# Front pairs of a two-layer hybrid trunk: which steps stand behind the casts in the queues, and when the S1 tiles of the next pair are loaded

## The chip, the cores and the metric

The kernel runs on one core of one Trainium2 chip. A time is the device time of one execution in microseconds (us), and it is the median over several executions. A core has five engines with a queue each: TensorE (PE, matmuls, with the weight loads shown as PEld), VectorE (DVE), ScalarE (ACT), GpSimd (POOL) and SyncE (SP, which here only issues DMAs). Each works through its queue in the order written, and an instruction that waits for a semaphore holds up all behind it.

## The reference

Two layers, a sequence of 512 tokens, width 2048, float32. In each layer one projection `h @ w_in` gives all heads' inputs and gates, and one projection `@ w_out` brings their outputs back:

```
h = rmsnorm(x, g_pre)
z = h @ w_in
gq, gk, gv, gg, ga, aq, ak, av, ag = split_columns(z)
log_a = log_sigmoid(ga @ w_alpha + b_alpha) / 16
o_gla = rmsnorm(gla_chunk_causal(gq, gk, gv, log_a)) * silu(gg)
o_att = rmsnorm(chunk_band_attention(aq, ak, av, rel_bias)) * silu(ag)
y = concatenate([o_gla, o_att]) @ w_out
return x + rmsnorm(y, g_post)
```

## The kernel before

**Matmuls.** [...] For a weight tile the cast is made on ScalarE (`high`, `wh`, line 251) and the subtraction on VectorE (`low`, `wl`, line 257).

**Pairs.** Two blocks of 512 columns of `w_in` make a pair. Instead of eight block products, a pair takes seven (P1 to P7, after Strassen), of sums of weight blocks and of sums of token blocks. Each product is cut along the inner dimension into four jobs, c = 0 to 3, of 512 KB of weights and 12 matmuls. P5 and P6 add two weight tiles on VectorE first (line 240). The token sums S1 to S4 are made once per layer (`make_sums`, additions on line 764), split, and written to DRAM; P5 multiplies S1, P6 S2, P3 S4, P7 S3 and P4 A22.

**Front pairs.** Three pairs of each layer come first: pair 0 (AG0, AG1), pair 1 (GG0, GG1) and pair 2 (AV0, AV1). Their P1 and P2 form a head that needs no token sums:

```
HEAD = (("P1", 0), ("P1", 1), ("P2", 0), ("P2", 1), ("P1", 2), ("P2", 2))
```

Meanwhile the token steps, a generator that is advanced `rate` times a job (`pump`), prepare the token columns: in layer 0 each chunk is scaled by `g_pre` half on ScalarE and half on VectorE (lines 718 and 716), then split into high and low (lines 113 and 114). Then, pair by pair, come P5, the mixture of P6 and P3 (`MIDDLE`: P6 c0, P3 c0, P6 c1, P3 c1, P6 c2, P6 c3, P3 c2, P3 c3), P7 and P4.

**Copies between banks.** P1's result stays in PSUM banks "X", and is copied out (`copies("p1")`, line 432) before P2 adds onto the same banks. Before P4, the X banks are copied onto the Y banks (line 534), and P4 adds onto these. For P7's last and P4's first job the matmuls go token tile by token tile.

**Preparing ahead.** After a job, `ahead()` prepares the next: weight loads up to five jobs ahead, casts up to four, lows up to three, and loads of token sums (`bring`, line 230) up to four. Weight tiles lie in rings of four; a load waits until the tile four before it has been read.

**Order.** A scheduler places the instructions of each engine by a simulation of the program, by readiness, and by program order among those that are ready. The kernel adds edges: `issue_after(i)` puts an instruction behind `i` on its engine. `behind()` does that with the second to last cast and the second to last low traced so far, where the flag is set:

```
if in_front[0] and len(casts) > 1 and len(lows) > 1:
    with tc.issue_after(casts[-2]), tc.issue_after(lows[-2]):
        yield
```

All token steps go through it while `in_front[0]` is true, that is in all three front pairs, and so does `close`, what is done with a finished product (the copies too).

**S1 tiles.** Pairs 1 and 2 read S1 back from DRAM, 512 KB for each c, into four slots (g8, g11, g14, g15) used in turn by P5 c0 to c3, then by P6 c0, P3 c0, P6 c1 and P3 c1, then by the next pair's P5. `bring_next` issues those of the next pair after P7 c0 to c3, each behind the last weight load traced. The forget gate's steps (its last has lines 900 to 902) run beside pair 1 at `rate=0.25`.

Of the kernel before, what the change touches and what calls it, by code (L numbers as in the profile page):

```python
# [35 lines left out]
def hybrid_trunk(  # L36
# [13 lines left out]
    nc = tc.nc  # L50
# [85 lines left out]
    C_IN, C_END = (0, 1, 2, 3), (2, 3, 0, 1)  # L136
    MIDDLE = (("P6", 0), ("P3", 0), ("P6", 1), ("P3", 1), ("P6", 2), ("P6", 3), ("P3", 2), ("P3", 3))

    def products(cs, *names):
        return [(p, c) for p in names for c in cs]  # L140

    def middle(cs):
        return [(p, cs[i]) for p, i in MIDDLE]
# [5 lines left out]
    def early_rest(cs):  # L149
        return products(cs, "P5") + middle(cs) + products(cs, "P7", "P4")  # L150
# [11 lines left out]
    in_front = [False]  # L162

    @contextmanager
    def behind():
# [3 lines that stand above are left out]
        else:  # L169
            yield  # L170
# [94 lines left out]
    stream, infos_of = [], []  # L265
# [24 lines left out]
    def take(l, blk, kind, c):  # L290
        i = cursor[0]
        job = stream[i]
        assert (job.l, job.b0, job.kind, job.c) == (l, blk, kind, c)
        for what in ("load", "bring", "high", "low"):
            prepare(what, i + 1)
        cursor[0] += 1
        return job

    def ahead():
        i = cursor[0]  # L300
        for what, n in (("load", 3), ("high", 3), ("low", 3), ("load", 4), ("high", 4), ("load", 5), ("bring", 4)):
            if what in ("high", "low") and all(z.kind == "std" for z in stream[i + n - 2 : i + n]):
                n -= 1
            prepare(what, i + n)
# [26 lines left out]
    def drain():  # L331
        while tasks or delayed:
            pump(1)
# [72 lines left out]
    class Pair:  # L406
# [104 lines left out]
        def run(self, prods, rate=0.0, skip=0, after=None):  # L511
            pace = Pace(rate, skip)
            for k, c in prods:
                job = take(self.l, self.b0, k, c)
                self.matmuls(job, k, c)
                ahead()
                if c == self.last:
                    with behind():
                        self.close(k)
                if after is not None:  # L520
                    after(k, c)
                pace()

        def close(self, k):
            if k == "P1":
                self.copies("p1", self.acc["X"])
            elif k == "P5":
                self.copies("p5", self.acc["Y"])
            elif k == "P6":
                self.copies("x", self.acc["X"])  # L530
            else:
                if k == "P7" and self.seeded:
                    for t in range(2):
                        nc.scalar.copy(self.acc["Y"][t], self.acc["X"][t])  # L534
                for t in range(2):
                    self.finished(k, t)
                if k == "P7" and self.early and not self.seeded:
                    self.copies("x", self.acc["X"])
# [119 lines left out]
    def turn_norms():  # L658
        while turns:
            turns.pop(0)()  # L660
            yield
# [193 lines left out]
    def layer(l):  # L855
# [10 lines left out]
        def gate_consume(half):  # L866
            def f(j, h, t, src, comb):
                z = settled(src, comb)
                until(lambda: (l, h) in normed)
                gate(half, j, 2 * h + t, z, inv_rms(l, 2 * h + t))  # L870
            return f
# [97 lines left out]
        def av_consume(j, h, t, src, comb):  # L969
# [14 lines left out]
        front = [  # L984
            Pair(l, FRONT[0], gate_consume(1), scaled=False, **how),
            Pair(l, FRONT[1], gate_consume(0), scaled=False, x_bank=2, **how),
            Pair(l, FRONT[2], av_consume, keep=early_kept, **how),
        ]
        in_front[0] = True
        for n, (k, i) in enumerate(HEAD):  # L990
            front[i].run(products(C_IN, k), rate=2.7 if n < 2 and l == 0 else 1.9)
        if l == 0:
            tasks[0] = beside(tasks[0], first_norms(1), 2)
            tasks.append(load_forget_gate(0))
        tasks.append(turn_norms())
        def bring_next(i):
            def f(k, c):
                if k == "P7":
                    next(z for z in stream if z.pair is infos_of[l][i] and (z.kind, z.c) == ("P5", c)).bring()
            return f  # L1000

        front[0].open(0)
        front[0].run(early_rest(C_IN), rate=1.0, after=bring_next(1))
        drain()
        tasks.append(forget_gate())
        front[1].open(2)
        front[1].run(early_rest(C_IN), rate=0.25, after=bring_next(2))
        drain()
        act_table("natural_log_exp_and_others")
        av[0, 0] = slot(AVT[0][0], [2, 512])  # L1010
# [505 lines left out]
    for l in range(L):  # L1516
        layer(l)
# [57 lines left out]
```

## Time and profile before

| | |
|---|---|
| median of 3 runs | 1615.48 us (1614.38 to 1619.49) |
| profiled execution | 1618.52 us, span of its instructions 1616.7 us |
| TensorE busy | 1590.8 us (98%) |
| VectorE, ScalarE, GpSimd busy | 78%, 57%, 11% |
| DMA | 467.83 MB, mean 289 GB/s |
| TensorE's mean granted clock | 0.997 |

The span runs from the first to the last instruction. A row of the timeline gives start, duration, engine, line, operation, and output<-inputs by the program's names; in brackets stands how long the engine was idle before it and what released it. In layer 0 the front pairs take about the first 256 us, in layer 1 about the stretch from 811 to 1056 us.

### The profile page before, as it was taken

The page shows a single profiled execution, that of the slowest core. Times are in us where ns is not written, and L with a number is a line of the kernel's source. Part 1 is how long each engine was busy: PE and PEld are TensorE (multiplying, and loading weights), DVE is VectorE, ACT ScalarE, POOL GpSimd, SP SyncE. Part 2 cuts the span into 40 slices and gives each one's busy share as a digit, 9 for nine tenths or more (in the row PEclk, how much of TensorE's full clock was granted, in tenths as well). Part 3 has the DMA queues.
Part 4 walks back from the last instruction along what each step waited for, and adds up shares of the span by engine and source line. Part 5 has one row for each costly group of instructions (what it writes and reads, how often), then busy time and mean ns, then how long its engine had stood idle before and what let it go on. Part 6 is the DMA issues. An engine that isn't in the chain of part 4 may idle for free.

```text
span 1616.7 us, 24522 instructions
## 1 busy us (share of the span) xinstructions
PE 1590.8 (98%) x8818; PEld 1355.4 (84%) x8818; DVE 1257.7 (78%) x1580; ACT 923.4 (57%) x1534; POOL 181.5 (11%) x302
## 2 busy tenths in 40 slices
PE   8999999999999999999999999999999999999997
PEld 5787879999988887788887877899999888777886
DVE  6788787786877876778868878768778868866886
ACT  7575454456676544555675555445566765445543
POOL 1141000000101101310212100000000011013100
PEclk9999999999999999999999999999999999999999
DMA  9989777867868698799878789678588676979996
GB/s 365 370 282 363 287 244 260 294 208 270 294 212 288 225 344 308 269 379 331 344 242 322 282 313 340 227 244 298 184 310 295 213 273 237 356 240 342 374 322 223
DMA packets 150617, 467.83 MB, mean 289 GB/s; under 512 B 16492, under 2 KB 35956, under 8 KB 150496
## 3 DMA queue, kind: packets, MB, share of 16 engines
q1 hardware_dynamic: 127232, 385.79, 67.6%
q0 software_dynamic: 22688, 79.53, 12.8%
q8 instruction: 69, 1.13, 0.3%
q10 hardware_dynamic: 576, 0.95, 0.2%
q14 instruction: 52, 0.43, 0.1%
HBM read 393.01 MB, written 72.11 MB: 288 GB/s over the span
## 4 chain that ended last, share of the span: by engine, by line
PE 92%; DMA 4%; DVE 2%; issue 1%; ACT 1%; SPq 0%; DVEq 0%; POOLq 0%; ACTq 0%
PE mm L504 49%; PE mm L491 20%; PE mm L380 11%; DMA H<-in_w_dram 3%; PE ax L1087 2%; PE ax L504 1%; DMA raw<-in_w_dram 1%; PE ax L1070 1%; PE ax L1253 1%; PE ax L1287 1%; DVE wl L257 1%; PE ax L1049 1%; PE ax L1050 1%; PE ax L686 1%; PE ax L1048 1%
## 5 line engine op out<-in xcount | busy, mean ns | idle before, releaser
L251 ACT CAST wh<-raw 128x1024 fp32r<-128x1024 f32 x256 | 269.4, 1053 | 237.9 <-PE mm L504 111.5
L257 DVE TENSOR_TENSOR wl<-raw,wh 128x1024 fp32r<-128x1024 f32 x256 | 312.5, 1222 | 115.2 <-PE mm L504 43.0
L251 ACT CAST wh<-H 128x1024 fp32r<-128x1024 f32 x239 | 251.0, 1052 | 230.1 <-PE mm L504 88.0
L257 DVE TENSOR_TENSOR wl<-H,wh 128x1024 fp32r<-128x1024 f32 (+1 forms) x241 | 292.8, 1217 | 101.7 <-PE mm L504 44.0
L504 PE MATMUL mm<-wh,sa 128*128 128x512 f32 x1088 | 345.3, 392 | 2.0 <-ACT mm L534 2.0
L504 PE MATMUL mm<-wh,g 128*128 128x512 f32 x832 | 259.2, 391 | 0.0
L504 PEld LDWEIGHTS mm<-wh,sa 128*128 128x128 f32 x1088 | 203.2, 188 | 45.7 <-ACT mm L534 2.9
L491 PE MATMUL mm<-sa,wh 128*128 128x256 f32 x1280 | 235.9, 285 | 0.0
L504 PE MATMUL mm<-wh,a 128*128 128x512 f32 x704 | 229.4, 397 | 6.3 <-ACT a L113 5.2
L504 PE MATMUL mm<-wl,sa 128*128 128x512 f32 x544 | 212.5, 391 | 0.0
L240 DVE TENSOR_TENSOR H<-H,raw 128x1024 f32<-128x1024 f32 x160 | 194.2, 1220 | 18.3 <-DMA raw<-in_w_dram 9.0
L491 PEld LDWEIGHTS mm<-sa,wh 128*128 128x128 f32 x1280 | 199.3, 192 | 0.3
L504 PEld LDWEIGHTS mm<-wh,g 128*128 128x128 f32 x832 | 156.8, 189 | 32.7 <-ACT wh L251 0.3
L491 PE MATMUL mm<-sa,wl 128*128 128x256 f32 x640 | 181.0, 283 | 0.0
L504 PE MATMUL mm<-wl,g 128*128 128x512 f32 x416 | 163.2, 392 | 7.3 <-DVE wl L257 7.3
L504 PEld LDWEIGHTS mm<-wh,a 128*128 128x128 f32 x704 | 132.0, 189 | 39.5 <-ACT a L113 6.2
L504 PE MATMUL mm<-wl,a 128*128 128x512 f32 x352 | 138.8, 394 | 0.6 <-DVE wl L257 0.6
L491 PEld LDWEIGHTS mm<-sa,wl 128*128 128x128 f32 x640 | 122.3, 191 | 0.1
L504 PEld LDWEIGHTS mm<-wl,sa 128*128 128x128 f32 x544 | 102.2, 188 | 20.9
L504 PEld LDWEIGHTS mm<-wl,g 128*128 128x128 f32 x416 | 78.4, 189 | 26.5 <-DVE wl L257 10.1
L491 PE MATMUL mm<-a,wh 128*128 128x256 f32 x512 | 94.3, 285 | 0.0
L551 POOL TENSOR_TENSOR sm<-sm,cst 128x4 f32<-128x4 f32 (+2 forms) x40 | 49.0, 1225 | 326.6 <-DVE sm L1447 131.7
(208 smaller groups left out, 2271.9 us busy)
## 6 DMA issues: line engine op xcount, KB each, us to landing
raw<-in_w_dram SPq DMA_DIRECT2D x352, 512.0 KB, 5.5
sa<-S SPq DMA_DIRECT2D x128, 512.0 KB, 4.5
H<-in_w_dram SPq DMA_DIRECT2D x63, 512.0 KB, 5.9
S<-g POOLq DMA_DIRECT2D x32, 512.0 KB, 5.8
g<-S SPq DMA_DIRECT2D x32, 512.0 KB, 5.8
sa<-A SPq DMA_DIRECT2D x32, 512.0 KB, 5.9
oS<-g POOLq DMA_DIRECT2D x32, 512.0 KB, 6.1
sa<-oS SPq DMA_DIRECT2D x32, 512.0 KB, 5.1
```

What stands on the lines that cost most here:

```text
L240: nc.vector.tensor_tensor(out=h, in0=h, in1=r, op=ALU.add)
L251: last_cast[0] = nc.scalar.copy(self.wh, src).ins
L257: last_low[0] = nc.vector.tensor_tensor(out=self.wl[:, kk, :], in0=self.src[:, kk, :], in1=self.wh[:, kk, :].bitcast(F32), op=ALU.subtract ...
L380: mm = nc.tensor.matmul(pss[o], a[:, part, t], rhs[:, kk, :], start=(i == 0 and kk == 0 and m == 0), stop=(i == n - 1 and kk == 1 and m == 2),
L491: nc.tensor.matmul(dst, lhs[:, kk, f], a[:, part, tok], start=(fresh and kk == 0 and m == 0 and ft % 2 == 0), stop=(c == self.last and kk ...
L504: nc.tensor.matmul(out_ps[t], a[:, part, tok], rhs[:, kk, :], start=(fresh and kk == 0 and m == 0), stop=(c == self.last and kk == 1 and m ...
L551: return nc.gpsimd.tensor_tensor(out=out_r, in0=v, in1=mhalf[:, : v.shape[-1]], op=ALU.pow).ins
L686: mm = nc.tensor.matmul(gate_ps[l][g : g + 32, half * 256 : (half + 1) * 256], gate_w[l][:, kh * 8 + c * 2 + kk, :], full[half, c][:, kh, ...
L1048: nc.tensor.matmul(ps[:, :n], self.qh[:, t], self.kh[:, :n], start=True, stop=False)
L1049: nc.tensor.matmul(ps[:, :n], self.qh[:, t], self.kl[:, :n], start=False, stop=False)
L1050: nc.tensor.matmul(ps[:, :n], self.ql[:, t], self.kh[:, :n], start=False, stop=True)
L1087: nc.tensor.matmul(o, self.pt[i][:, j * P : (j + 1) * P], av[hd // 4, j // 2][:, j % 2, (hd % 4) * P : (hd % 4 + 1) * P], start=(j == 0), ...
```

## The change

1. The flag `in_front[0]` is set only from the third entry of the head on in layer 0 (in layer 1 from the first, as before). So in layer 0 the token steps beside P1 of pairs 0 and 1, eight jobs, get no edge.
2. The copies of P1's result and those of X onto Y before P4 move out of `close` and ahead of it, so they get no edge.
3. The S1 loads of the next pair are issued elsewhere: for pair 1 after P5 c1, P6 c0, P7 c0 and P7 c1 of pair 0; for pair 2 after P6 c1, P6 c2, P6 c3 and P3 c3 of pair 1.
4. The rate beside pair 1 goes from 0.25 to 0.4.

```
@@ run
                 if c == self.last:
+                    if k == "P7" and self.seeded:
+                        for t in range(2):
+                            nc.scalar.copy(self.acc["Y"][t], self.acc["X"][t])
+                    if k == "P1":
+                        self.copies("p1", self.acc["X"])
                     with behind():
                         self.close(k)
@@ close
-            if k == "P1":
-                self.copies("p1", self.acc["X"])
-            elif k == "P5":
+            if k == "P5":
                 self.copies("p5", self.acc["Y"])
             elif k == "P6":
                 self.copies("x", self.acc["X"])
-            else:
-                if k == "P7" and self.seeded:
-                    for t in range(2):
-                        nc.scalar.copy(self.acc["Y"][t], self.acc["X"][t])
+            elif k != "P1":
                 for t in range(2):
                     self.finished(k, t)
@@ layer
-        in_front[0] = True
         for n, (k, i) in enumerate(HEAD):
+            in_front[0] = l > 0 or n > 1
             front[i].run(products(C_IN, k), rate=2.7 if n < 2 and l == 0 else 1.9)
...
-        def bring_next(i):
+        def bring_next(i, times):
             def f(k, c):
-                if k == "P7":
-                    next(z for z in stream if z.pair is infos_of[l][i] and (z.kind, z.c) == ("P5", c)).bring()
+                if (k, c) in times:
+                    nxt = ("P5", times.index((k, c)))
+                    next(z for z in stream if z.pair is infos_of[l][i] and (z.kind, z.c) == nxt).bring()
             return f
 
         front[0].open(0)
-        front[0].run(early_rest(C_IN), rate=1.0, after=bring_next(1))
+        front[0].run(early_rest(C_IN), rate=1.0, after=bring_next(1, [("P5", 1), ("P6", 0), ("P7", 0), ("P7", 1)]))
         drain()
         tasks.append(forget_gate())
         front[1].open(2)
-        front[1].run(early_rest(C_IN), rate=0.25, after=bring_next(2))
+        front[1].run(early_rest(C_IN), rate=0.4, after=bring_next(2, [("P6", 1), ("P6", 2), ("P6", 3), ("P3", 3)]))
         drain()
```

## The prediction

> **What bounds the kernel now.** I read the page first: is any engine full?
>
> ```profile
> span 1616.7 us, 24522 instructions
> PE 1590.8 (98%) x8818; PEld 1355.4 (84%) x8818; DVE 1257.7 (78%) x1580; ACT 923.4 (57%) x1534; POOL 181.5 (11%) x302
> ```
>
> TensorE is the bound and the change removes no matmul. All that can be won is 1616.7 - 1590.8 = 25.9 us of idle TensorE, and what a lowered clock costs. So the second view is who TensorE waited for (total us, times, longest):
>
> ```profile
> PE mm L504 <- DVE wl L257: 7.9, 7, 2.0
> PE mm L504 <- ACT a L113: 5.2, 1, 5.2
> PE mm L504 <- ACT mm L534: 2.0, 2, 1.5
> ...
> PE mm L504 <- ACT pc L432: 0.4, 1, 0.4
> ```
>
> Third, the timeline of TensorE gives the place of each (start, duration, then the idle time before it and its releaser):
>
> ```profile
> 15.54 0.80 PE L504 MATMUL mm<-wh,a 128*128 128x512 f32 x1 [5.24 <-ACT a L113]
> ...
> 128.98 0.50 PE L504 MATMUL mm<-wl,g 128*128 128x512 f32 x1 [0.46 <-DVE wl L257]
> 133.09 0.50 PE L504 MATMUL mm<-wh,sa 128*128 128x512 f32 x1 [1.54 <-ACT mm L534]
> 149.16 0.50 PE L504 MATMUL mm<-wl,g 128*128 128x512 f32 x1 [1.73 <-DVE wl L257]
> ...
> 205.31 0.50 PE L504 MATMUL mm<-wl,g 128*128 128x512 f32 x1 [0.99 <-DVE wl L257]
> 211.82 0.50 PE L504 MATMUL mm<-wl,g 128*128 128x512 f32 x1 [0.31 <-DVE wl L257]
> ...
> 947.12 0.50 PE L504 MATMUL mm<-wl,g 128*128 128x512 f32 x1 [2.05 <-DVE wl L257]
> 1004.11 0.50 PE L504 MATMUL mm<-wl,g 128*128 128x512 f32 x1 [1.80 <-DVE wl L257]
> ```
>
> All lie in the front pairs of the two layers, in the code that is changed. Fourth, the windows show clock and DMA there (length, busy us of PE, PEld, DVE, ACT, POOL, then clock, DMA share, GB/s):
>
> ```profile
> 12.00:20.00 8.00, 4.46 (x14) 3.62 (x15) 6.40 (x12) 6.37 (x13) 0.00 (x0) 0.79 1.03 403
> 20.00:36.00 16.00, 16.00 (x72) 13.12 (x70) 11.73 (x17) 16.00 (x28) 3.55 (x8) 1.00 1.04 400
> 92.00:100.00 8.00, 8.00 (x37) 6.64 (x36) 8.00 (x9) 8.00 (x18) 5.59 (x2) 1.00 0.33 102
> 100.00:148.00 48.00, 45.43 (x199) 36.51 (x197) 37.16 (x40) 24.53 (x33) 14.17 (x26) 1.00 1.00 368
> 164.00:172.00 8.00, 8.00 (x37) 6.60 (x37) 5.59 (x6) 3.84 (x5) 0.00 (x0) 1.00 0.27 76
> 184.00:204.00 20.00, 20.00 (x90) 16.51 (x88) 14.88 (x15) 8.66 (x11) 1.62 (x3) 1.00 1.00 392
> 1004.00:1012.00 8.00, 7.89 (x28) 6.37 (x29) 7.94 (x9) 7.41 (x10) 1.65 (x3) 0.79 0.90 314
> ```
>
> Ahead of each stalled change of pair the DMA is full (1.00); shortly before that it stands mostly idle (0.33, 0.27). At 90 matmuls in 20 us a product of 12 takes 2.7 us; that is the clock for "jobs ahead" below.
>
> **The change part by part.** It adds and removes no instruction; it changes places in queues.
>
> *1. Token steps at the start.* ScalarE, then VectorE, then SyncE's issues:
>
> ```profile
> 9.21 1.05 ACT L251 CAST wh<-H 128x1024 fp32r<-128x1024 f32 x1 [0.89 <-DMA H<-in_w_dram]
> 11.20 1.04 ACT L251 CAST wh<-H 128x1024 fp32r<-128x1024 f32 x1 [0.94 <-DMA H<-in_w_dram]
> 13.12 1.04 ACT L251 CAST wh<-H 128x1024 fp32r<-128x1024 f32 x1 [0.88 <-DMA H<-in_w_dram]
> 14.07 0.90 ACT L718 ACTIVATE g<-g,gcol 128x256 f32<-128x256 f32 x2
> 14.88 1.12 ACT L113 CAST a<-g 128x512 fp32r<-128x512 f32 x2
> ...
> 12.28 1.22 DVE L257 TENSOR_TENSOR wl<-H,wh 128x1024 fp32r<-128x1024 f32 x1 [0.76 <-ACT wh L251]
> 13.42 0.61 DVE L716 TENSOR_SCALAR g<-g,gcol 128x256 f32<-128x256 f32 x2
> ...
> 3.06 0.43 SPq L607 DMA_DIRECT2D g<-in_xt_dram  x1
> 3.54 0.43 SPq L180 DMA_DIRECT2D H<-in_w_dram  x1
> ```
>
> When the steps after job 0 are traced, the casts to job 4 and the lows to job 3 have been; the second to last of each are the cast of job 3 and the low of job 2. Exactly behind these stand the token steps (14.07 behind 13.12; 13.42 behind 12.28): the ordering binds. The columns of chunk 1 (issued at 3.06) stand right ahead of the weights whose cast begins at 11.20, and behind those cast at 9.21, so I put their landing at about 10, an estimate. Freed, chunk 1 fits behind the first of these casts: 10.26, one g (about 0.5), one a (about 0.6) give 11.4, and its low on VectorE ends at about 12.0. TensorE would restart at 12.0, not 15.54: 3.5 us. Bounds: nothing, if the scheduler still takes the casts first, since they come earlier in program order; and 5.2 us, when the slow clock goes too: (1 - 0.79) x 8 = 1.7 us. I take 3.5, near the upper end but without the clock, because DMA (1.04) and ScalarE (16.00 of 16) are full until 36 us and the next weights can't follow much further. Below nothing: a token step placed ahead of a cast holds it, in order, until its columns land; ScalarE's waits above, up to 0.94 us each, are the nearest rows.
>
> *2. The copies that P4 and P2 wait for.*
>
> ```profile
> 131.50 1.05 ACT L251 CAST wh<-H 128x1024 fp32r<-128x1024 f32 x1 [2.56 <-DVE H L240]
> 132.45 1.06 ACT L534 COPY mm<-mm 128x512 f32<-128x512 f32 x2
> ```
>
> ScalarE waited 2.56 us for that cast's input while the copies stood behind it. Freed, the copy of the first bank runs while the second is still being multiplied (P7's last product goes tile by tile): the 1.54 us go, and layer 1's 2.0 - 1.5 = 0.5. Late next is the cast, by the copies' 1.06 us; it is three jobs, 8 us, ahead of its use. Bounds: 0 to 2.0, or 1.06 lost at a place where the cast is needed at once. For P2 (line 432) the row says 0.4 at most; I take it.
>
> *3. The S1 loads of pair 1.*
>
> ```profile
> 121.48 0.37 SPq L230 DMA_DIRECT2D g<-S  x1
> ...
> 128.20 0.49 SPq L230 DMA_DIRECT2D g<-S  x1
> ...
> 146.74 1.23 DVE L240 TENSOR_TENSOR H<-H,raw 128x1024 f32<-128x1024 f32 x1 [2.72 <-DMA H<-in_w_dram]
> ...
> 64.06 1.29 DVE L764 TENSOR_TENSOR g<-g,g 128x512 f32<-128x512 f32 x2
> ```
>
> First and last of the four. P7's last product ends at 131.5 (133.09 - 1.54); 15 and 11 jobs back, P5 c1 ends near 91 to 93 and P6 c0 near 101, so c0 and c1 move into or next to the idle stretch; c2 and c3 move two jobs, within the full one. So 2 x 0.52 MB leave it: 1.05 MB at 392 GB/s = 2.7 us by which the weights of the add at 146.74 land sooner. Stalls there are 0.46 + 1.54 + 1.73 = 3.7; since TensorE comes sooner by what part 2 saves, both parts together give what the DMA gives, 2.7 (bounds 0 and 3.7). Layer 1 has 0.5 + 2.05 = 2.5, which I take whole (bounds 0 and 2.5). In SyncE's queue each load moves past some ten weight loads, and those behind it wait if its slot isn't free; slots g8 and g11 are read last by the token sums' additions, whose last row is 64.06.
>
> *4. The S1 loads of pair 2, and rate 0.4.* All four go from behind P7 to behind P6 and P3, 3 to 7 jobs or 8 to 19 us sooner, into and around the stretch with share 0.27: up to 2.1 MB or 5.3 us leave the full one ahead of 205 us, against stalls of 0.99 + 0.31 = 1.3 in layer 0 and 1.8 in layer 1. The faster pace also takes the forget gate's last step out of VectorE's line at that place:
>
> ```profile
> 203.45 0.68 DVE L900 TENSOR_TENSOR g<-ax,t 96x512 f32<-96x512 f32 x1
> ```
>
> Behind it waits the low that TensorE waits for: 0.7 us of the stall alone. I take all, 1.3 + 1.8 (bounds: 0.7 a layer, by this step only, and all).
>
> *5. The clock.* Right behind the 1.80 us stall the clock falls: (1 - 0.79) x 8 = 1.7 us. Without the stall I count them gained (bounds 0 and 1.7).
>
> **Sum.** 3.5 + 2.7 + 0.4 + 2.5 + 1.3 + 1.8 + 1.7 = 13.9. The profiled execution took 1618.5 (1.8 around its span), 3.0 above the median of the runs shown: 1618.5 - 13.9 = 1604.6. Against the median, if that run has no slow stretch in layer 1: 1615.5 - 12.2 = 1603.3. I forecast 1604.5.
>
> **The rivals.**
> A. The start stays as it is, because the casts come first by program order, too. For: the casts were traced first. Against: the token steps stand right at their bound, so they were ready no later. 1604.5 + 3.5 = 1608.0.
> B. The changes of pair stay bound by the DMA. For: from 100 to 148 us its share is 1.00, and a TensorE that comes 3.5 us sooner asks sooner. Then of the 9.7 us outside the start and the P2 copies some 3 remain, an estimate (part 4's floors of 0.7 each and the 1.5 of part 2): 1618.5 - 3.5 - 0.4 - 3 = 1611.6. Against: 0.33 and 0.27.
> C. Neither start nor pairs gain; 0 to 3 us: 1614 to 1617.
> E. The slow stretch near 1005 us comes whatever the gap before it. For: the 2.05 us gap ahead of 947.12 is longer, and behind it the clock is 1.00:
>
> ```profile
> 948.00:952.00 4.00, 4.00 (x19) 3.30 (x18) 4.00 (x5) 3.61 (x6) 1.06 (x2) 1.00 1.02 347
> ```
>
> That gives 1604.5 + 1.7 = 1606.2. [...] The trace speaks against it at 1004, with the clock down right behind 1.80 us.
> D. The other side: an early S1 load waits in SyncE's queue for a slot that TensorE still reads, and the weight loads behind it come late.
>
> ```profile
> SPq L230 <- PE mm L504: 11.0, 6, 3.4
> ...
> raw<-in_w_dram SPq DMA_DIRECT2D x352, 512.0 KB, 5.5
> ```
>
> The first row (80 to 216 us) shows such waits, up to 3.4 us. Weights are prepared three jobs ahead, 8.1 us, less 5.5 to land and 2.3 for cast and low: a hold over about 0.3 us reaches TensorE. At four changes of pair 4 x 3.1 = 12.4 would be lost and no pair term gained: 1618.5 - 3.9 + 12.4 = 1627. Against: at each new place the slot's last product is two or more jobs back.
>
> **How the numbers follow.** Forecast 0.39 (own range 1600 to 1606), A 0.20, E 0.08, B 0.17, C 0.09, D 0.07. Range 1600 to 1613: its low end is every front stall gone (5.24 + 3.73 + 1.30 in layer 0, 0.4 + 0.5 + 2.05 + 1.80 in layer 1, 15.0 in all) and both slow stretches (3.4), 1618.5 - 18.4; its high end takes in B. Faster is under 1610.6, 0.3% of 1615.5, about what a measurement of this kernel can tell: forecast, E, most of A, half of B: 0.73. Same: the rest of A and B, and C: 0.20. Slower: D, 0.07.
>
> **What would show it.** Part 1: the idle before the matmul at 15.54 shrinks under 2 us and L718 stands ahead of the third cast. Part 2: no wait on line 534. Parts 3 and 4: L230 loads near 93, 101 and 160 to 176 us, a DMA share there well above 0.33, no wait over 1 us on line 257 at the first products of pairs 1 and 2, L900 well ahead of 200 us. Part 5: clock 1.00 around 1005 us. I would be wrong if SyncE's L230 rows wait long for TensorE (D), if the casts between 16 and 36 us come later than now, or if a new wait stands where an old one was.

## The result, and the profile after

The changed kernel takes 1607.93 us (median of 6 runs, 1606.70 to 1609.82), the kernel before 1616.72 us on the same chip (6 runs, 1614.38 to 1619.49): a ratio of 0.9945, 95% interval [0.9932, 0.9959]. That is 8.8 us sooner; 1604.5 had been forecast. The profiled execution took 1606.85 us. It ran 1.1 below its median and the profiled one of before 1.8 above its own, so the two traces differ by 11.9 us in span (1616.7 to 1604.8), not by 8.8. All times here are of executions at a granted clock of 0.994 or more; one of the kernel with the loads in their old place, 1968.35 us at 0.752, is left out.

TensorE's idle time fell from 25.9 to 17.2 us. The page, and the view of who TensorE waited for (total us, times, longest):

```profile
span 1604.8 us, 24518 instructions
PE 1587.6 (99%) x8818; PEld 1353.8 (84%) x8818; DVE 1257.0 (78%) x1580; ACT 923.2 (58%) x1534; POOL 184.8 (12%) x302
```

```profile
PE mm L504 <- ACT wh L251: 2.1, 2, 1.6
PE mm L504 <- ACT mm L520: 1.8, 2, 0.9
PE mm L504 <- DVE wl L257: 1.7, 3, 0.7
...
PE mm L504 <- ACT a L113: 1.2, 2, 1.0
```

The large lines of before have shrunk, those of the lows (a low is a weight tile less its cast) from 7.9 to 1.7 and the start's from 5.2 to 1.2. The copies onto the Y banks (now line 520) still have 1.8 of 2.0, and the first line is new, but for 0.6 us on a cast of the first jobs. The timeline of TensorE has the places:

```profile
10.31 0.73 PE L504 MATMUL mm<-wh,a 128*128 128x512 f32 x2 [0.99 <-ACT a L113]
25.20 0.50 PE L504 MATMUL mm<-wl,a 128*128 128x512 f32 x1 [0.50 <-DVE wl L257]
30.99 0.73 PE L504 MATMUL mm<-wh,a 128*128 128x512 f32 x2 [0.49 <-ACT wh L251]
...
73.73 0.73 PE L504 MATMUL mm<-wh,a 128*128 128x512 f32 x2 [1.62 <-ACT wh L251]
74.98 0.50 PE L504 MATMUL mm<-wl,a 128*128 128x512 f32 x1 [0.52 <-DVE wl L257]
130.24 0.50 PE L504 MATMUL mm<-wh,sa 128*128 128x512 f32 x1 [0.85 <-ACT mm L520]
...
924.90 0.50 PE L504 MATMUL mm<-wh,sa 128*128 128x512 f32 x1 [0.95 <-ACT mm L520]
```

No stall is left at a change of pair: those of 0.46, 1.73, 0.99, 0.31, 2.05 and 1.80 us are gone. The windows:

```profile
12.00:20.00 8.00, 8.00 (x37) 6.58 (x36) 5.96 (x10) 6.31 (x11) 0.00 (x0) 1.00 1.03 403
60.00:76.00 16.00, 13.86 (x60) 10.86 (x59) 7.80 (x10) 7.28 (x9) 1.09 (x2) 1.00 1.01 401
92.00:100.00 8.00, 8.00 (x37) 6.64 (x36) 7.53 (x9) 8.00 (x18) 3.83 (x8) 1.00 0.74 233
100.00:148.00 48.00, 47.15 (x208) 38.59 (x208) 42.78 (x44) 28.25 (x36) 12.53 (x22) 1.00 0.99 365
164.00:172.00 8.00, 8.00 (x37) 6.64 (x36) 6.57 (x7) 4.76 (x6) 0.00 (x0) 1.00 0.59 199
1004.00:1012.00 8.00, 8.00 (x37) 6.64 (x36) 3.68 (x3) 3.06 (x3) 0.00 (x0) 1.00 0.41 147
```

The DMA's empty stretches are in use (0.33 became 0.74, 0.27 became 0.59), and the clock is 1.00 from 12 to 20 us and from 1004 to 1012 us, where it was 0.79.

To see what each place contributed, I matched TensorE's matmuls of the two traces by their order and subtracted start times: the lead of the new kernel, in us, at the end of each stretch. Here and below, a lead "at 31 us" is that of the matmul that starts at 31 us in the kernel before; the rows shown go by their own kernel's time.

| stretch | foreseen | change of the lead | lead after it |
|---|---|---|---|
| start, to 31 us (24 us in the changed kernel's time) | 3.5 | +6.55 | 6.55 |
| rest of the P1 heads and the token steps, to 62 us | 0 | -2.4 | 4.1 |
| P2 of pair 2, 70 to 81 us | 0.4 | -2.7 | 1.4 |
| pair 0 to pair 1, to 153 us | 2.7 | +3.45 | 4.85 |
| pair 1 to pair 2, to 219 us | 1.3 | +1.95 | 6.8 |
| rest of layer 0, and layer 1's P2 | 0 | -0.6 | 6.2 |
| layer 1, pair 0 to 1 | 2.5 | +2.0 | 8.2 |
| layer 1, pair 1 to 2, with the clock | 1.8 + 1.7 | +3.7 | 11.9 |

The pairs came out close to the sum. The start did not: it gained more than foreseen and then handed most of it back by 81 us. ScalarE's queue at that place, in the kernel before and then in the changed one:

```profile
70.83 1.06 ACT L251 CAST wh<-raw 128x1024 fp32r<-128x1024 f32 x1 [0.86 <-PE mm L504]
73.55 1.06 ACT L251 CAST wh<-raw 128x1024 fp32r<-128x1024 f32 x1 [1.66 <-PE mm L504]
75.14 0.59 ACT L432 COPY pc<-mm 128x512 f32<-128x512 f32 x1 [0.53 <-PE mm L504]
```

```profile
71.01 0.59 ACT L432 COPY pc<-mm 128x512 f32<-128x512 f32 x1 [5.44 <-PE mm L504]
72.14 0.59 ACT L432 COPY pc<-mm 128x512 f32<-128x512 f32 x1 [0.54 <-PE mm L504]
72.63 2.94 ACT L251 CAST wh<-raw 128x1024 fp32r<-128x1024 f32 x3
```

The freed copies of P1's result now stand ahead of three casts. ScalarE waits 5.44 us for P1's last product with the casts behind it, then does all three in a row, and TensorE waits 1.62 us for the first of them and 0.52 us for its low.

### The profile page after: what moved, and what is told of

It is laid out like the page before. It is cut to its first block, busy times and chain, and to the rows that moved or that the text cites. A ratio compares the mean times of both kernels' runs of the same rounds, so it can differ in the third digit from the quotient of the medians.

```text
span 1604.8 us, 24518 instructions
## 1 busy us (share of the span) xinstructions
PE 1587.6 (99%) x8818; PEld 1353.8 (84%) x8818; DVE 1257.0 (78%) x1580; ACT 923.2 (58%) x1534; POOL 184.8 (12%) x302
## 4 chain that ended last, share of the span: by engine, by line
PE 94%; DMA 2%; DVE 1%; ACT 1%; issue 1%; SPq 0%; DVEq 0%; POOLq 0%; ACTq 0%
PE mm L504 53%; PE mm L491 20%; PE mm L380 9%; PE ax L1088 2%; PE ax L504 1%; DMA t<-fg 1%; PE ax L1071 1%; PE ax L1288 1%; PE ax L1254 1%; DMA raw<-in_w_dram 1%; PE ax L686 1%; PE ax L1050 1%; PE ax L1051 1%; PE ax L1049 1%; DVE wl L257 1%
## 5 line engine op out<-in xcount | busy, mean ns | idle before, releaser
L551 POOL TENSOR_TENSOR sm<-sm,cst 128x4 f32<-128x4 f32 (+2 forms) x40 | 56.7, 1418 | 318.9 <-DVE sm L1448 126.4
```

The source lines that it names most:

```text
L551: return nc.gpsimd.tensor_tensor(out=out_r, in0=v, in1=mhalf[:, : v.shape[-1]], op=ALU.pow).ins
```

## The experiments

"Before" and "after" are the two kernels, and the changes are numbered as in the section on the change. Each ratio is to the kernel before on the same chip.

**The start alone.** Before, with change 1 only:

```
+            in_front[0] = l > 0 or n > 1
```

> The kernel before with part 1 alone (no edge for the token steps beside the first eight jobs). Theory: the start's 5.24 us wait falls to about 1 us and the slow clock behind it goes, so TensorE is 6.5 us ahead at the tenth job; about 2.4 us of that are lost by 50 us (waits for casts at 25 and 31 us, gate products); since P1's copies stand behind the casts as before, nothing is lost near 74 us, so about 4 us are left when pair 0 ends. The old waits of the pair changes stay (line 534 near 1.5 us, line 257 1 to 2 us each). Time about 1616.7 - 4 = 1612.7. Rival (the DMA is the limit of the first 150 us): the waits at the first change of pair grow by what was won, and the time is that of before within 1 us.

Measured: 1616.88 us against 1617.62, ratio 0.9989 [0.9979, 0.9999]. The lead is 5.9 us at 31 us, 3.5 at 62, 2.5 at 81, 1.7 at 109 and 1.2 at 134. The first 2.4 us of the loss are the short waits and the gate products described for after further down. From 62 us on it is a chain of waits of 0.51 to 1.55 us; TensorE's timeline has, among others:

```profile
73.41 0.50 PE L504 MATMUL mm<-wh,a 128*128 128x512 f32 x1 [0.65 <-ACT pc L432]
...
147.28 0.50 PE L504 MATMUL mm<-wl,g 128*128 128x512 f32 x1 [1.06 <-DVE wl L257]
```

The second row is the stall that stood at 149.16 before, with 1.73 us. TensorE comes to it 1.2 us sooner and the low is there 1.9 us sooner, so 1.06 us of waiting are left. By the medians the gain at the start is worth some 0.7 us by itself, and the interval allows 0.2 to 3.4. The profiled execution ended 4.4 us ahead, but it ran 2.5 us below its own median, so how much of the start stays for good is not settled.

**The loads and the rate alone.** Before, with changes 3 and 4 only:

```
+        def bring_next(i, times):
...
+        front[0].run(early_rest(C_IN), rate=1.0, after=bring_next(1, [("P5", 1), ("P6", 0), ("P7", 0), ("P7", 1)]))
+        front[1].run(early_rest(C_IN), rate=0.4, after=bring_next(2, [("P6", 1), ("P6", 2), ("P6", 3), ("P3", 3)]))
```

> The kernel before with parts 3 and 4 alone (S1 loads earlier, rate 0.4), no part 1 and no part 2. Theory: the waits on line 257 at the four changes of pair go (1.73 + 1.3 in layer 0, 2.05 + 1.80 in layer 1) with the slow clock behind the last (1.7): 8.6 us, 1608 in a run that has the slow stretch and about 1609.5 against the median. The start keeps 5.24 us and the copies before P4 keep 1.54 and 0.48. Rival (the relief came from the start being earlier): at most the last step of the forget gate, 0.7 a layer, 1615.

Measured: 1609.83 us, ratio 0.9952 [0.9938, 0.9966], nearly the whole change's 0.9945. Who TensorE waited for:

```profile
PE mm L504 <- ACT a L113: 5.1, 1, 5.1
PE mm L504 <- ACT mm L534: 2.1, 2, 1.5
...
PE mm L504 <- DVE wl L257: 0.5, 1, 0.5
```

The lows' 7.9 us are 0.5, with the start and the copies as they were.

**The loads in their old place.** After, with change 3 undone (the rate stays 0.4):

```
-        ... after=bring_next(1, [("P5", 1), ("P6", 0), ("P7", 0), ("P7", 1)]))
+        ... after=bring_next(1, [("P7", 0), ("P7", 1), ("P7", 2), ("P7", 3)]))
-        ... after=bring_next(2, [("P6", 1), ("P6", 2), ("P6", 3), ("P3", 3)]))
+        ... after=bring_next(2, [("P7", 0), ("P7", 1), ("P7", 2), ("P7", 3)]))
```

> The changed kernel with the S1 loads back behind P7 c0 to c3 (parts 1, 2 and rate 0.4 stay). Theory: the loads make most of the gain; the waits on line 257 at the four changes of pair return, 1 to 2 us each, the later of layer 1 with or without a slow stretch of 1.7: 1607.9 + 5 to 7, about 1614. Rival: rate 0.4 and the copies made it; the time stays under 1610.

Measured: 1618.15 us against 1617.97, ratio 1.0003 [0.9994, 1.0012]. The whole gain is gone. TensorE's timeline and the windows:

```profile
147.53 0.50 PE L504 MATMUL mm<-wl,g 128*128 128x512 f32 x1 [1.41 <-DVE wl L257]
...
944.47 0.73 PE L504 MATMUL mm<-wh,g 128*128 128x512 f32 x2 [0.60 <-ACT wh L251]
946.85 0.50 PE L504 MATMUL mm<-wl,g 128*128 128x512 f32 x1 [1.65 <-DVE wl L257]
```

```profile
92.00:100.00 8.00, 8.00 (x37) 6.64 (x36) 7.58 (x9) 8.00 (x17) 7.06 (x4) 1.00 0.42 111
...
947.00:951.00 4.00, 4.00 (x11) 3.13 (x12) 4.00 (x4) 3.60 (x6) 1.08 (x2) 0.57 0.96 351
```

The DMA's share from 92 to 100 us is 0.42 again, the stalls at the changes of pair are back, and nothing is won there: the lead, 6.7 us at 31 us and 1.5 at 81 much as in after, is 1.0 at 219 us, where after has 6.8. With the loads and the rate alone nearly the whole gain comes, and without the moved loads none of it: the S1 loads carry the gain.

**The rate alone undone.** After, with 0.25 beside pair 1:

```
-        front[1].run(early_rest(C_IN), rate=0.4, ...
+        front[1].run(early_rest(C_IN), rate=0.25, ...
```

> The changed kernel with the rate beside pair 1 back at 0.25 (the loads stay moved). Theory: with the weights landing early the forget gate's last step is hidden wherever it stands: 1607.9 within 0.7. Rival: line 900 stands ahead of the low that TensorE waits for, 0.7 us in each layer: 1609.3.

Measured: 1611.06 us, ratio 0.9960 [0.9947, 0.9973], 3.1 us above after's median, 2.4 by the two ratios, whose intervals overlap. In the trace, the lead over before falls by 2.7 us from 190 to 204 us of before, where after's does not move. First TensorE's timeline, then VectorE's:

```profile
197.37 0.51 PE L504 MATMUL mm<-wl,sa 128*128 128x512 f32 x1 [0.86 <-DVE wl L257]
```

```profile
193.34 1.23 DVE L240 TENSOR_TENSOR H<-H,raw 128x1024 f32<-128x1024 f32 x1 [2.90 <-issue]
...
198.37 0.68 DVE L900 TENSOR_TENSOR g<-ax,t 96x512 f32<-96x512 f32 x1
198.97 2.35 DVE L257 TENSOR_TENSOR wl<-H,wh 128x1024 fp32r<-128x1024 f32 x2
```

At the old rate the gate's last step again stands in front of two lows of pair 1's end, but only one of TensorE's three waits here, 0.30 us at 200.24, lies behind it. The other two, 0.31 us at 187.02 and the 0.86 shown, end before line 900 starts. In front of the 0.86 stands the addition at 193.34, which in after starts at 188.83. The load of its weight tile was issued at 187.00 (182.54 in after), and in both kernels the addition starts 6.3 us behind that issue. So the rate also decides when weight loads go out; which of the gate's steps holds this one back stays open. My floor of 0.7 us for this step was too low: the old rate costs 2.7 us in layer 0 of this trace and nothing in layer 1 (there the lead grows from 2.6 to 8.4 us, as after's does from 6.0 to 11.9).

**P1's copies back behind the casts.** After, with the P1 copies inside the ordered part again:

```
-                    if k == "P1":
-                        self.copies("p1", self.acc["X"])
                     with behind():
+                        if k == "P1":
+                            self.copies("p1", self.acc["X"])
                         self.close(k)
```

> The changed kernel with the copies of P1's result back behind the casts (parts 1, 3, 4 and the P4 copies stay). Theory: freed, the two copies of pair 2 in layer 0 stand ahead of three casts on ScalarE and hold them until TensorE is through with P1; put back, the waits at 73.7 and 75.0 us (1.62 + 0.52, 2.7 us of lead in all) go and the lead is kept to the end: about 1607.9 - 2.7 = 1605.2. The wait of P2 in layer 1 goes from 0.2 back to 0.4. Rival (the weights land late there, at 76 us): waits of 1.5 us or more stay near 74 us, on line 257 or 251, and the time is 1607 to 1608.

Measured: 1606.66 us, ratio 0.9933 [0.9921, 0.9945]; after's 0.9945 lies at the end of that interval. The wait for casts at 73 us is gone and the lead at 81 us is 3.6 instead of 1.4 us. But it is 4.3 against after's 4.85 at 153 us, and 12.1 against 11.9 at the end. TensorE's timeline:

```profile
72.31 0.50 PE L504 MATMUL mm<-wh,a 128*128 128x512 f32 x1 [0.56 <-ACT pc L432]
...
130.80 0.50 PE L504 MATMUL mm<-wh,sa 128*128 128x512 f32 x1 [1.70 <-ACT mm L520]
```

So the freed copies do cause the 2.1 us of waiting at 73 us, but in the trace all that is saved there is paid again before 153 us: 0.68 us at 98.26 for a copy that stands behind ScalarE's squares, 0.57 on a low at 126.50, and 1.70 instead of 0.85 at P4's copies.

**P4's copies ahead of the casts too.** The kernel just above, with P7's copies onto the Y banks traced ahead of `ahead()`; `ahead()` leaves the casts and lows of two jobs out after P7 c2, and those cast after P7 c3 get an edge behind the copies (`last_evac`):

```
...
+                seed = k == "P7" and self.seeded and c == self.last
+                if seed:
+                    for t in range(2):
+                        last_evac[0] = nc.scalar.copy(self.acc["Y"][t], self.acc["X"][t]).ins
+                hold[0] = self.seeded and (k, c) == ("P7", C_IN[-2])
                 ahead()
...
```

> The kernel of the run before this one, and the casts and lows of the jobs P4 c2 and c3 are traced only behind P7's last job and put behind the copies of X onto Y. Theory: not the edge but the cast of P4 c2 ahead of the copies, which waits for its sum on VectorE, makes P4 wait; with the copies first, the 0.85 and 0.95 us go: 1.8 us less than that run, about 1603.4. Rival: the two casts, two jobs ahead of their use instead of four, come late, and P4 c2 waits for line 251 or 257 as long as P4 c0 waited for the copies: the same time as that run, or up to 2 us more.

Measured: 1604.76 us, ratio 0.9922 [0.9909, 0.9934], 1.9 us below the kernel above, as expected. ScalarE's timeline:

```profile
128.51 0.57 ACT L525 COPY mm<-mm 128x512 f32<-128x512 f32 x1 [1.48 <-PE mm L510]
129.67 0.57 ACT L525 COPY mm<-mm 128x512 f32<-128x512 f32 x1 [0.59 <-PE mm L510]
130.15 1.06 ACT L251 CAST wh<-H 128x1024 fp32r<-128x1024 f32 x1
```

Here each copy runs as soon as its bank is done, the first beside the second bank's products. TensorE does not wait for them any more in either layer. In after, the order on ScalarE was the one of before:

```profile
128.65 1.05 ACT L251 CAST wh<-H 128x1024 fp32r<-128x1024 f32 x1 [2.56 <-DVE H L240]
129.60 1.06 ACT L520 COPY mm<-mm 128x512 f32<-128x512 f32 x2
```

**The gate products in one visit.** Between 24 and 54 us of its own time after lost 2.5 us of its lead. Three short waits there are 1.16 us in sum. The rest I put down to the gate products (line 686), 64 small matmuls of which TensorE does a few between the jobs: 7 visits in before, 8 in after. By the distances of the matmuls' starts the visits cost 7.9 us in after and 7.1 in before, and the slower starts behind two of the waits another 0.5. The kernel with P1's copies behind the casts, with all 64 traced behind the last chunk:

```
-                if half and ch < 4:
-                    gate_products(0, (ch,))
+            if half:
+                gate_products(0, (3, 2, 1, 0))
+                yield
```

> The changed kernel with P1's copies behind the casts, and layer 0's 64 small products of the forget gate (line 686) chained so that TensorE does them nearly in one run, not in eight visits between jobs. Theory: each visit costs TensorE some 0.3 us beside the products themselves, so of the lead of 6.1 us at the ninth job that fell to 4.3 by 50 us in the kernel with P1's copies behind, 1.5 us or more stay; the end is then bound by ScalarE near 98 us (P5's copies behind the squares), where that kernel already waited 0.68, so the end gains under 0.5. Rival: the 1.75 us are waits for token columns, not visits; the lead at 50 us stays 4.3.

Measured: 1610.12 us, one run. TensorE's timeline shows the visits, and ScalarE's what happened 30 us later:

```profile
40.85 0.63 PE L686 MATMUL ax<-g,ev 128*32 128x256 f32 x4
...
43.91 3.65 PE L686 MATMUL ax<-g,ev 128*32 128x256 f32 x60
...
74.01 0.54 PE L504 MATMUL mm<-wh,a 128*128 128x512 f32 x1 [3.81 <-ACT pc L432]
```

```profile
72.43 1.04 ACT L251 CAST wh<-raw 128x1024 fp32r<-128x1024 f32 x1 [3.58 <-DMA raw<-in_w_dram]
73.38 1.06 ACT L432 COPY pc<-mm 128x512 f32<-128x512 f32 x2
```

TensorE makes two visits. The lead is 6.7 us at 54 us of its own time instead of 4.5: six visits fewer save 2.9 us (23.23 against 26.12 us for the same matmuls, with 0.35 us more of waiting), 0.5 us each. Then a cast waits 3.58 us for weights, the copies behind it with it, and TensorE 3.81 us; a stretch of slow clock follows (0.57 from 74 to 78 us) and the lead is 0.3 us at 81 us. The same edit on the kernel with P4's copies first:

> The kernel with P4's copies first and P1's copies behind, and the gate's products in one run. Theory: what the start keeps more is lost again to ScalarE near 99 us: within 0.5 of that kernel's 1604.8. Rival: the lead is kept, 1603.0.

Measured: 1607.38 us, ratio 0.9940 [0.9927, 0.9953], against 0.9922 [0.9909, 0.9934] without the edit: the same wait, 4.03 us at 74.1 us, and a mean granted clock of 0.997 in the profiled execution, 0.999 without the edit. Between 60 and 76 us the DMA's share is 1.03 in the kernel with P1's copies behind the casts and 0.99 in the same kernel with the edit. TensorE comes sooner with the edit, but its weights do not: the last cast ahead of P1's copies starts at 72.43 us with it, behind 3.58 us of waiting for the DMA, and at 70.73 us without it.

**What holds the lead between 70 and 110 us.** Three kernels on the one with P4's copies first: the x rows of the second half (2 MB) loaded five weight loads later; the first norms of that half at every 4th token step, which takes their squares on ScalarE out of 90 to 98 us; and both.

```
-        if i in (5, 7, 22, 23):
+        if i in (5, 7, 27, 28):
...
-            tasks[0] = beside(tasks[0], first_norms(1), 2)
+            tasks[0] = beside(tasks[0], first_norms(1), 4)
```

> The kernel with the P4 copies first (median 1604.8), with the loads of the x rows of the second half (2 MB) moved from the 23rd and 24th weight load of layer 0 to the 28th and 29th. Theory (the DMA's share of about 1.0 between 60 and 76 us is what takes the start's lead back): the weights of P2 c1 and c2 land sooner, the wait of 0.98 at 73.1 us for the P1 copies goes, and the lead over before, 4.1 at 70 us, is still 3.9 at 98 us instead of 2.7; then the full ScalarE (0.73 at 99 us) takes its part. Time 1603.6. Rival 1 (the sum that the DMA has to bring before pair 1 is the same, only later): the wait turns up between 76 and 150 us, lead 3.7 to 3.8 after the change to pair 1 as before, time 1604.8. Rival 2: the rows come too late for the token sums' first norms, and the token steps behind them hold P5: slower, 1606 or more.

> The kernel with the P4 copies first (median 1604.8), with the first norms of the second half advanced at every 4th token step instead of every 2nd, so that their squares on ScalarE (line 563 of before) come later than 90 to 98 us. Theory (ScalarE, full from 90 to 98 us, takes 0.7 to 1.0 us of the lead at 99 us): the wait for ev at 99 us goes, lead 2.7 instead of 1.7 at 109 us, and the time is 1603.8. Rival 1: the DMA, full from 100 us on, takes the microsecond at the change to pair 1: same lead as now after 150 us (5.8), 1604.8. Rival 2: the squares come to stand in front of casts of P5 to P7: new waits on wh, 1605.5 or more.

> Both edits of the two kernels beside it on the kernel with the P4 copies first (median 1604.8): x rows of the second half at the 28th and 29th weight load, and the first norms at every 4th step. Theory: no wait over 0.3 us from 60 to 110 us, the lead of 4.1 at 62 us is still 4.0 at 110 us (1.7 without the edits), and all of the 2.3 stays: 1602.5. Rival: the DMA, full from 100 to 148 us, hands out the weights of pair 1 at the same time as before, the lead after 150 us is 5.8 as without the edits, and the time 1604.8.

| kernel | us | ratio | lead at 70 | 98 | 109 | 153 us | end |
|---|---|---|---|---|---|---|---|
| P4's copies first | 1604.76 | 0.9922 [0.9909, 0.9934] | 4.1 | 2.7 | 1.7 | 5.8 | 14.5 |
| x rows later | 1606.04 | 0.9925 [0.9905, 0.9945] | 3.9 | 3.2 | 1.4 | 6.1 | 12.4 |
| norms slower | 1604.31 | 0.9923 [0.9906, 0.9939] | 4.4 | 3.7 | 3.7 | 5.95 | 14.5 |
| both | 1604.41 | 0.9918 [0.9903, 0.9932] | 3.4 | 2.6 | 2.6 | 7.2 | 14.1 |

The times cannot be told apart. The traces can. Slower norms do take the wait at 99 us away (lead at 109 us 3.7 instead of 1.7), and then it is taken back before pair 1, as the first rival said, at a low and at P4's copies: TensorE's timeline of that kernel has

```profile
125.74 0.50 PE L510 MATMUL mm<-wl,g 128*128 128x512 f32 x1 [0.85 <-DVE wl L257]
...
128.90 0.50 PE L510 MATMUL mm<-wh,sa 128*128 128x512 f32 x1 [0.60 <-ACT mm L525]
```

and its lead at 153 us is 5.95 against 5.8. The later x rows alone only move the wait, to 1.38 us on a low at 99.3 us, and of the 6.1 us at 153 they keep 5.55. With both edits TensorE is busy without a break from 100 to 148 us, and the lead at 153 us is the largest, 7.2 us:

```profile
100.00:148.00 48.00, 48.00 (x213) 39.62 (x212) 41.51 (x43) 29.07 (x42) 13.40 (x25) 1.00 0.94 352
```

Of that 1.4 us more, layer 1 returned all in the profiled execution (among others a wait of 0.9 us at 867 us). What sets that part of layer 1 was not tried.

Three versions thus have lower medians than both kernels: 1604.3 to 1604.8 us against after's 1607.9, ratios of 0.9918 to 0.9923 to before, with intervals that reach at most 0.0007 into after's. The simplest is the one with P4's copies first.

## Why the prediction was right, and where its steps failed

The time lies 3.4 us above the forecast and inside its range; 8.8 us were gained of the 11.0 that 1604.5 meant against the median then known. The sign and the main mechanism, S1 loads moved into an idle stretch of the DMA, were right; the sum was right in part by luck, since errors cancelled.

- *Part 1, the start, 3.5.* The mechanism was right and its size at the spot too low: the idle before the first matmul of chunk 1 fell from 5.24 to 0.99 us, and with it went the slow clock behind (0.79 to 1.00), 6.55 us. TensorE restarted at 10.31, not at 12.0: I had put the landing of the columns at about 10, and the split of chunk 1 began at 9.63. The step that failed is the one that took this term as final. It did not last, and not for the reason I gave for taking no more, DMA and ScalarE full until 36 us: 2.4 us went by 62 us, in short waits and to the gate products, and 2.7 by 81 us, most of it by part 2's own copies. The net of the start to 81 us is 1.4 us in after, and 0.7 us in the time of the start alone.
- *Part 2, the P2 copies, 0.4.* Wrong in sign at one place: -2.7 us at 73 to 81 us in layer 0, by the casts that now stand behind the copies. I had named "late next is the cast" for P4 and priced it at nothing, three jobs ahead; at P2 the casts were not three jobs ahead: with the copies back behind them, the same three ran at 66.5, 68.6 and 70.7 us, the first two after waits for their weights, and P2 starts at 72.3. The step lacked ScalarE's 5.44 us of waiting in front of a cast. It cost little in the end: the kernel without this edit is 1.3 us faster by the medians and 1.9 by the ratios, with intervals that overlap.
- *Part 2, the P4 copies, up to 2.0.* This step failed. The wait was 2.0 and is 1.8. "The copies stood behind it" was read rightly from the row, but the edge was not what put them there: without it the order on ScalarE is the same. The cast is traced first, so that program order alone would do it. Only the kernel that traces the copies first and holds the casts back moved them, and there 1.9 us came.
- *Part 3, 2.7 and 2.5; part 4, 1.3 and 1.8.* Right in kind and near in size: +3.45, +2.0, +1.95 and, with the clock, +3.7. The floor of part 4 was mis-sized: the rate is worth 2.7 us in layer 0, not 0.7, and only a part of that by line 900. Line 900 now ends at 170 us:

```profile
169.58 0.68 DVE L900 TENSOR_TENSOR g<-ax,t 96x512 f32<-96x512 f32 x1
```

- *Part 5, the clock, 1.7.* Without the 1.80 us stall the slow stretch at 1004 us did not come (1.00 from 1004 to 1012 us, where it was 0.79); rival E did not happen in this trace.
- *Rival A* did not happen at the start. *Rival B* was half right: the changes of pair are not bound by the DMA once the loads are moved, but its argument ("asks sooner") holds at another stage: with the gate products in one visit TensorE comes to 74 us 6.7 us ahead and waits 3.8 to 4.0 us, behind casts that wait for the DMA. The 9.7 us in its sum are 10.0, which changes nothing. *Rival D* did not happen: in after, SyncE's S1 loads wait 14.4 us for TensorE in 9 waits from 80 to 216 us, where it was 11.0 in 6, and the longest is shorter:

```profile
SPq L230 <- PE mm L504: 14.4, 9, 2.9
```

## What to carry to other kernels

A stall that ends on a late transfer was mended here where the DMA stood idle some tens of us earlier (shares of 0.33 at 92 and 0.27 at 164 us, for stalls at 149 and 205 us); look for that window first, and price the move by the bytes that leave the full stretch (for pair 1 in layer 0 1.05 MB at 392 GB/s, 2.7 us; 3.45 us came). A gain ahead of a stretch in which the DMA is full may be only lent (with the gate products in one visit a lead of 6.7 us became 0.3): follow the lead, matmul by matmul, through the next full stretch before counting it. Taking an ordering edge away changed ScalarE's in-order queue only where the edge was binding (at P4's copies the order stayed, and 1.8 of 2.0 us of waiting with it), and the copies so freed stood in front of three casts and held them through a wait of 5.44 us: read the rows behind such an instruction, too.

## What the runs showed of the hardware

**The clock behind an idle TensorE.** The idle times are those of TensorE's timeline, the granted clock is that of the windows:

| kernel | idle time before the matmul that starts at | granted clock behind it |
|---|---|---|
| before | 5.24 us, 15.54 | 0.79 from 12 to 20 us |
| before | 1.73 us, 149.16 | 1.00 from 148 to 152 us |
| before | 2.05 us, 947.12 | 1.00 from 948 to 952 us |
| before | 1.80 us, 1004.11 | 0.79 from 1004 to 1012 us |
| after | 0.99 us, 10.31 | 1.00 from 12 to 20 us |
| after | 1.62 us, 73.73 | 1.00 from 72 to 80 us |
| the loads in their old place | 0.60 us, 944.47, and 1.65 us, 946.85 | 0.57 from 947 to 951 us |
| the gate products in one visit | 3.81 us, 74.01 | 0.57 from 74 to 78 us |

In the kernel before, each of these two falls went to 0.50 and lasted 3.4 us, from 15.1 to 18.5 us and from 1005.0 to 1008.4 us. The window behind the gap of 3.81 us:

```profile
74.00:78.00 4.00, 3.99 (x11) 3.16 (x12) 0.73 (x1) 0.66 (x2) 0.00 (x0) 0.57 1.03 410
```

The length of a gap alone doesn't sort these: behind 1.80 us the clock fell, behind 2.05 us it did not. So the length of a gap, by which rival E went, does not settle it, and part 5 was right with some luck: why 1.80 us was enough and 2.05 us was not, nothing here tells.

I tried gaps made on purpose, on the kernel with P4's copies first:

```
-                    for t in range(2):
+                    for t in (0, 1, 0, 0, 0, 0):
                         last_evac[0] = nc.scalar.copy(self.acc["Y"][t], self.acc["X"][t]).ins
```

> The kernel with the P4 copies first, with the copy of the first X bank onto its Y bank done five times instead of once: behind P7's last product of each front pair (six places) TensorE then idles about 2.5 us (4 x 0.57, and what a start after a wait takes). It asks what makes the clock fall behind an idle TensorE. [...] Time: 1604.8 + 6 x 2.3 + 1.7 for each slow window, 1618.6 for none, 1625 for four, 1629 for six, less what waits for weights absorb.

Measured: 1611.32 us, one run, and inconclusive. TensorE waited 0.7 us at most at each of the six places instead of 2.5, since the copies ran on beside P4's matmuls (3.40 us of them from 128.08 us on, P4 from 129.84), and the mean granted clock was 0.999, as in the profiled execution without this edit. No run shows the four or six slow windows that the forecast counts:

```profile
PE mm L510 <- ACT mm L525: 4.0, 6, 0.7
```

**Visits.** A visit of small matmuls between large ones cost TensorE about 0.5 us: the same matmuls took 26.12 us with 8 visits (P1's copies behind the casts) and 23.23 us with 2 (the same kernel with the gate products in one visit), 2.9 us for six visits.
